# Rotary angles ahead of the masks on GpSimd, a key copy moved back, merged transfers, high products first in the up-projection

## The chip, the cores and the metric

The kernel runs on one core of a Trainium2 chip. Five engines work side by side, each through its own row of instructions in order: TensorE (PE: matmuls and transposes; PEld is its loading of weights), VectorE (DVE), ScalarE (ACT), GpSimd (Pool) and SyncE (SP, which here only issues transfers). An instruction waits for semaphores that other engines or transfers raise, and what stands behind it on its engine waits with it.

The metric is the device time in microseconds (us). The kernel before took 402.79 us, the median of three runs (402.75, 402.79 and 403.62). The times inside the program come from one profiled execution.

## What is computed

One decoder layer on 256 tokens of width 1024: RWKV-7 time mixing and an attention branch with rotary angles run on one normalised input, are merged with gates, projected, and followed by a gated MLP with a short convolution. Cut to what the change touches:

```python
def partial_rope(x, positions):
    inv_freq = ROPE_THETA ** (-jnp.arange(half, dtype=jnp.float32) / half)
    ang = positions.astype(jnp.float32)[..., None] * inv_freq
    cos = jnp.cos(ang)[:, :, None, :]
    sin = jnp.sin(ang)[:, :, None, :]
    ...
def rwkv7_time_mix(z, ...):                       # kk: normalised keys
    kk = kk / jnp.maximum(jnp.sqrt(jnp.sum(kk * kk, axis=-1, keepdims=True)), 1e-12)
    def step(state, inp):                         # a scan over the tokens
        sa = jnp.einsum('bhvk,bhk->bhv', state, a_t)
        state = (state * w_t[:, :, None, :] + sa[..., None] * b_t[:, :, None, :]
                 + v_t[..., None] * k_t[:, :, None, :])
    ...
def conv_ffn(h, w_up, conv_w, conv_b, w_down):
    u = h @ w_up
    a, b = u[..., :D_FF], u[..., D_FF:]
    a = lax.conv_general_dilated(a, ...) + conv_b  # causal, 3 wide, per channel
    return (jax.nn.gelu(a, approximate=False) * b) @ w_down
```

## The kernel before

**Products in halves.** All weights and inputs are float32. The kernel splits each operand into a high part, rounded to the matmul's own format, and the low rest, and sums three products: high by high, high weight by low input, low weight by high input. Weights come in pieces of 128 x 1024 through SP into `raw` (four buffers). ACT (or DVE, three times) casts a piece to `whi` (L299, L301), DVE subtracts to get `wlo` (L310, three buffers), and TensorE takes both. `hx` holds the split input: `hh` and `hl`. In `wst` a piece with four blocks k gives, for each half m of the columns, eight high products (L346 with `hh`, L348 with `hl`, in turn) and then four low ones (L351).

**Order.** The first steps are written out by hand. Then two or three threads of work, written as generators (`chain` for RWKV-7, `bulk` for projections, gates and attention), hand over to each other by costs and delays that they name; a scheduler places each instruction, and `tc.issue_after(x)` puts one behind another. What comes out is one fixed row of instructions for each engine.

**Pool.** Early it makes `ident` and loads small parameters. `late_consts` then fills the constants: `bones`, `gmask`, `cmask` (L141), and `m16`, `m32` (L142 to L148), both shown as `m` in the profile. Behind them stands the arithmetic of the rotary angles in `rope_tables`: positions (`posi`) to float (`posf`, L208), times the frequencies `inv` (`ang`, L214), whole turns taken off in three steps (L218 to L228), clipped (L230). ACT makes `trig`, the sines and cosines, of `ang` (L232).

**DVE.** `masks` makes `rowf` from `ident` and multiplies `m16` by it (L154). This instruction was put behind the scan `L` (L666) with `issue_after`; on DVE it stands in front of `zs` (L414, the scaled output of a projection) and the `wlo` of the next weights. ACT and DVE make the keys `zk` from `zs` (L419, L420).

**RWKV-7.** ACT squares the keys (`sq`, L682), TensorE sums them (`pss`, L690), and the keys are normalised. DVE writes scaled keys into `KB` (L734, L737), which are transposed (`pk`, L761). Later the inverse of a triangular matrix is needed for chunks of 64 tokens; its blocks in `Xb` go through memory (`d`) into the block-diagonal `X` (L874, L879), which TensorE reads (`pp` L917, `px` L934).

**MLP.** For each of 11 groups j, `up()` makes two products: `acc`, from which `an` (L1482), `cv`, GELU and `hb` follow, and `at`, which multiplies `cv` (L1499). `down` (L1464 to L1468) adds the group's share to four sums `f0` to `f3`. In the first group `token_scale` works out the scale of the second norm: `rs` through ACT's square root (L1441), `rx` on DVE (L1443), and the transposes `prs` on TensorE (L1445).

Of the kernel before, what the change touches and what calls it, by code (L numbers as in the profile page):

```python
# [9 lines left out]
F32 = mybir.dt.float32  # L10
# [18 lines left out]
HALF = 8  # L29
# [8 lines left out]
def body(tc, x, positions, norm1_g, w_in, rwkv_mu, w_decay_up, decay_bias, w_aaa_up,  # L38
# [5 lines left out]
    with ctx:  # L44
# [25 lines left out]
        def acc(name="acc"):  # L70
            return ps.tile([128, 512], F32, name=name, tag="acc", bufs=3)
# [40 lines left out]
        def keep_warm(n):  # L112

            for _ in range(n):
                pe.matmul(idle[:, 0:256], ones[:, 0:128], ones[:, 0:256], start=True, stop=True)
# [16 lines left out]
        def late_consts():  # L132
            pool.memset(rst.rearrange("p (c i) -> p c i", i=64)[:, :, 0:1], 0.0)
            pool.memset(mhalf, -0.5)
            pool.memset(bones, 0.0)
            for q in range(2):
                pool.memset(bones[64 * q:64 * q + 64, 64 * q:64 * q + 64], 1.0)
            pool.tensor_copy(bonr, bones)
            pool.tensor_scalar(gmask[:, 0:64], jl[:, 0], 0.0, None, op0=OP.is_gt)
            pool.tensor_scalar(gmask[:, 64:128], jl[:, 1], 0.0, None, op0=OP.is_ge)  # L140
            pool.tensor_scalar(cmask, jp, 0.0, NEG, op0=OP.is_gt, op1=OP.mult)  # L141
            pool.memset(m16, 0.0)  # L142
            pool.memset(m32, 0.0)
            for q in range(4):
                o = 32 * (q % 2)
                pool.memset(m16[32 * q:32 * q + 32, o:o + 16], 1.0)
                if q % 2:
                    pool.memset(m32[32 * q:32 * q + 32, 0:32], 1.0)  # L148
# [22 lines left out]
        def col(i):  # L171
            return par[:, i:i + 1]
# [17 lines left out]
        loads += [(wdu[0:64], w_decay_up[0]), (wdu[64:128], w_aaa_up[0])]  # L190
        for i, g in enumerate((q_norm_g, k_norm_g)):
            loads.append((gqk[:, i], bass.AP(tensor=g.tensor, offset=g.offset, ap=[[0, 128], [1, 64]])))
        loads.append((posi, positions[0].rearrange("(t p) -> p t", p=128)))

        def small_loads(n, eng=None):
            for _ in range(n):
                (eng or nc.gpsimd).dma_start(*loads.pop(0))

        last_exp = []
        scans = []  # L200
        trig = cst.tile([128, 2, 2, HALF], F32, name="trig")
        turn = cst.tile([128, 2, 2, 2, 2, HALF], F32, name="turn")
        gcol = cst.tile([128, 1], F32, name="gcol")

        def rope_tables():
            ang = sb.tile([128, 2, 2, HALF], F32, name="ang")
            posf = sb.tile([128, 2], F32, name="posf")
            pool.tensor_copy(posf, posi)  # L208
            inv = sb.tile([128, HALF], F32, name="inv")
            fr = (500000.0 ** (-np.arange(HALF) / HALF)).astype(np.float32)  # L210
            for i in range(HALF):
                dve.memset(inv[:, i:i + 1], float(fr[i]))
            for t in range(2):
                pool.tensor_scalar(ang[:, 0, t], inv, posf[:, t:t + 1], None, op0=OP.mult)  # L214
            turns = sb.tile([128, 2, 2, HALF], F32, name="turns")
            part = sb.tile([128, 2, 2, HALF], F32, name="part")
            MAGIC = 12582912.0
            pool.tensor_scalar(turns[:, 0], ang[:, 0], 1.0 / (2 * math.pi), None, op0=OP.mult)  # L218
            pool.tensor_scalar(turns[:, 1], turns[:, 0], 0.25, None, op0=OP.add)
            pool.tensor_scalar(turns, turns, MAGIC, None, op0=OP.add)  # L220
            pool.tensor_scalar(turns, turns, MAGIC, None, op0=OP.subtract)
            c1 = 6.28125
            c2 = float(np.float32(round((2 * math.pi - c1) * 2 ** 20) / 2 ** 20))
            c3 = 2 * math.pi - c1 - c2
            pool.tensor_copy(ang[:, 1], ang[:, 0])
            for c in (c1, c2, c3):
                pool.tensor_scalar(part, turns, -c, None, op0=OP.mult)
                pool.tensor_tensor(ang, ang, part, op=OP.add)  # L228
            pool.tensor_scalar(ang[:, 1], ang[:, 1], math.pi / 2, None, op0=OP.add)
            pool.tensor_scalar(ang, ang, 3.1415925, -3.1415925, op0=OP.min, op1=OP.max)  # L230
            with tc.issue_after(last_exp[0]):
                act.activation(trig, ang, AF.Sin)  # L232
# [100 lines left out]
        def run(gen):  # L333
            for _ in gen:
                pass
# [87 lines left out]
        def first_steps():  # L423
# [13 lines left out]
            dve.memset(ones[:, 0:256], 1.0)  # L437
            dve.memset(eps1[:, 0:1], NORM_EPS)
            dve.memset(eps1[:, 1:2], N * NORM_EPS)
            keep_warm(12)  # L440
            pool.iota(jp, pattern=[[1, 128]], base=0, channel_multiplier=-1)
            pool.tensor_scalar(ident, jp, 0.0, None, op0=OP.is_equal)
# [3 lines left out]
            wdu_at = len(loads) - 5  # L446
            for _ in range(2):
                nc.sync.dma_start(*loads.pop(wdu_at))
            load_pair(early[1])
# [68 lines left out]
            both(2, 4)  # L518
            pool.memset(rst, 1.0)
            pool.memset(cmask, 0.0)  # L520
            pts.append(acc("xt").rearrange("p (k t c) -> p k t c", k=2, t=2))
            raw1, k1, c1 = raws.pop(0)
            hi1, lo1 = tiles("whi"), tiles("wlo")
# [79 lines left out]
        def ch16(t):  # L603
            return t.rearrange("p a (c i) -> p (a c) i", i=64)
# [43 lines left out]
        def chain():  # L648
# [30 lines left out]
            zk = zs["k"]  # L679
            sq = by("sq")  # L680
            for ct in range(4):
                act.activation(sq[:, ct], zk[:, ct], AF.Square, scale=col(KK_ + ct))  # L682
            yield 0, 4.5
            p = [chp("pss") for _ in range(2)]
            for t in range(2):
# [35 lines left out]
            def kbv(q, a):  # L721
                return KB[:, 64 * q:64 * q + 2048].rearrange("p (u a i) -> p u a i", a=2, i=64)[:, :, a]
# [8 lines left out]
            bb = av  # L731
            dve.tensor_tensor(flat(bb), flat(kk), flat(av), op=OP.mult)
            yield 0, 2.9
            dve.tensor_tensor(kbv(0, 1), ch16(bb), ch16(e3), op=OP.mult)  # L734
            for q, hs in PAR:
                with tc.issue_after(rqi):
                    last_k = dve.tensor_tensor(kbv(q, q)[hs], ch16(kp)[hs], ch16(e3)[hs], op=OP.mult).ins  # L737
                yield 0, 1.0
            yield from need("r", zs)
# [5 lines left out]

            G = [b8(f"G{q}", [128, 16, 128]) for q in range(2)]
            d1 = dr.tile([128, 256], F32, name="d1")
            d2 = dr.tile([8, 2, 16, 256], F32, name="d2")
# [112 lines left out]
            for n, o in ((4, 0), (4, 8), (8, 0)):  # L861
# [7 lines left out]
                if n == 4:  # L869
                    yield 0, 1.8  # L870
            dve.tensor_copy(Xb[:, 1, 0:256].rearrange("p (n i) -> p n i", n=16),
                            X0[:, 0:256].rearrange("p (i n) -> p n i", i=16))
            for xx in range(2):
                nc.sync.dma_start(d2[:, xx], Xb[:, xx, 0:256])  # L874

            def to_x(eng, side, x, us_, src):
                b = src[1]
                q0 = bsl(side).start + 16 * b
                eng.dma_start(X[q0:q0 + 16, x, us_, 16 * b:16 * b + 16],  # L879
                              d2[4 * src[0] + b, x, src[2]].rearrange("u (i n) -> i u n", i=16))  # L880

            for q in range(2):
                for b in range(4):
                    to_x((nc.sync, nc.gpsimd)[q], q, 0, slice(0, 16), (q, b, slice(0, 16)))
            for q in range(2):
                for b in range(4):
                    for a in range(2):
                        to_x((nc.sync, nc.gpsimd)[a], a, 1, slice(8 * q, 8 * q + 8), (q, b, slice(8 * a, 8 * a + 8)))

            def bank(nm):
                return chp(nm).rearrange("p (u n) -> p u n", u=8)
# [404 lines left out]
        def bulk():  # L1302
# [51 lines left out]
            while not last_exp:  # L1354
                yield 0, 0.5
            rope_tables()
            yield from queries()
# [91 lines left out]


        def up(bank=acc):
            p = bank()
            run(wst(p, 2, hh, hl))
            return p.rearrange("p (m s) -> p m s", m=2)

        def down(j, hb):
            for i in range(2):
                wh, wl = weights()
                st = j == 0 and i == 0
                for f in range(4):  # L1460
# [7 lines left out]
                    pe.matmul(fin[f], hb[:, 0, i, ts], wl[:, 0, cs], start=False, stop=False,  # L1468
                              skip_group_check=f == 3)

        prev = []
        for j in range(11):
# [81 lines left out]
```

## Time and profile before

| | us |
|---|---|
| median of the runs | 402.79 |
| the profiled execution | 402.01 |
| its span, first to last instruction | 400.2 |
| TensorE busy | 394.3 |
| VectorE busy | 301.9 |
| ScalarE busy | 237.3 |
| GpSimd busy | 49.5 |

The span lies 1.8 us below the time of the execution that it belongs to. In a row of a timeline the first number is the start in us, the second the time that it covers (that of several instructions where it ends in x2 or more); then come the engine, the line, the operation, what it writes and reads, and in brackets how long the engine stood idle before it and what ended that. Starts can lie a little before the end of the instruction ahead, since they overlap. In a list of waits the numbers are the total, the count and the longest. In the view of one tile, a row gives the shortest, median and longest duration in ns.

### The profile page before, as it was taken

To read this page: it belongs to the slowest core of one execution; us is meant where nothing else is said; L and a number is where in the kernel's file an instruction comes from. 1 tells how busy PE (TensorE), PEld (TensorE's weight loads), DVE (VectorE), ACT (ScalarE), POOL (GpSimd) and SP (SyncE) were. 2 spreads that over 40 slices of the span, in tenths; PEclk is the share of its full clock that TensorE was granted. 3 is DMA by queue.
4 is the path that set the end of the run, shared out by engine and by line. 5 is a ranking of instruction groups with operands and counts; after the bars stand their busy time and mean duration, and the time that the engine had idled before them with its cause. 6 is when DMAs were issued, how large, how long until landed. Compare 5 with 4: busy or idle time off the path is not lost.

```text
span 400.2 us, 9024 instructions
## 1 busy us (share of the span) xinstructions
PE 394.3 (99%) x3633; PEld 365.9 (91%) x3633; DVE 301.9 (75%) x508; ACT 237.3 (59%) x411; POOL 49.5 (12%) x87
## 2 busy tenths in 40 slices
PE   8999999999999999999999999999999999999996
PEld 6899999898999989999888999999999999999995
DVE  4989989899868989688875885765757667576583
ACT  5899477494747686635554874554545546455350
POOL 8888000010600021120000000000000000000000
PEclk9999999999999999999999999999999999999999
DMA  8943397554694333555661765666665565665612
GB/s 255 323 147 86 86 305 219 139 153 124 145 292 128 108 98 128 201 162 185 199 195 56 261 206 184 196 189 195 191 208 186 185 208 168 204 211 163 208 52 105
DMA packets 60589, 70.58 MB, mean 176 GB/s; under 512 B 7377, under 2 KB 51287, under 8 KB 60548
## 3 DMA queue, kind: packets, MB, share of 16 engines
q1 hardware_dynamic: 58116, 69.17, 56.1%
q10 hardware_dynamic: 1632, 0.59, 0.6%
q8 instruction: 28, 0.46, 0.5%
q0 software_dynamic: 800, 0.26, 0.4%
q14 instruction: 13, 0.11, 0.1%
HBM read 68.56 MB, written 1.44 MB: 175 GB/s over the span
## 4 chain that ended last, share of the span: by engine, by line
PE 85%; POOL 4%; DMA 4%; DVE 3%; ACT 1%; issue 1%; SPq 0%; POOLq 0%
PE acc L346 11%; PE acc L351 11%; PE acc L348 11%; PE at L351 5%; PE at L346 5%; PE at L348 5%; PE f L1468 5%; PE f L1466 5%; PE f L1464 5%; PE acc L367 4%; PE acc L371 4%; PE acc L368 4%; DMA posi<-in_positions_dram 2%; PE acc L1322 2%; PE pq L1323 1%; DMA p<-in_aaa_bias_dram 1%
## 5 line engine op out<-in xcount | busy, mean ns | idle before, releaser
L299 ACT CAST whi<-raw 128x1024 fp32r<-128x1024 f32 (+1 forms) x122 | 124.5, 1025 | 111.3 <-PE acc L348 44.0
L310 DVE TENSOR_TENSOR wlo<-raw,whi 128x1024 fp32r<-128x1024 f32 (+1 forms) x122 | 144.6, 1188 | 37.7 <-PE f L1468 14.4
L346 PE MATMUL acc<-hx,whi 128*128 128x256 f32 x400 | 99.4, 284 | 0.0
L348 PE MATMUL acc<-hx,whi 128*128 128x256 f32 x400 | 97.1, 279 | 0.0
L346 PEld LDWEIGHTS acc<-hx,whi 128*128 128x128 f32 x400 | 75.4, 188 | 2.4 <-issue 0.8
L348 PEld LDWEIGHTS acc<-hx,whi 128*128 128x128 f32 x400 | 75.4, 188 | 0.4
L351 PE MATMUL acc<-hx,wlo 128*128 128x256 f32 x400 | 62.3, 278 | 0.2 <-DVE rs L1440 0.2
L351 PEld LDWEIGHTS acc<-hx,wlo 128*128 128x128 f32 x400 | 53.2, 188 | 0.4 <-DVE wlo L310 0.4
L346 PE MATMUL at<-hx,whi 128*128 128x256 f32 x176 | 42.4, 278 | 0.0
L348 PE MATMUL at<-hx,whi 128*128 128x256 f32 x176 | 42.3, 277 | 0.0
L348 PEld LDWEIGHTS at<-hx,whi 128*128 128x128 f32 x176 | 33.1, 188 | 0.0
L346 PEld LDWEIGHTS at<-hx,whi 128*128 128x128 f32 x176 | 33.1, 188 | 0.0
L1468 PE MATMUL f<-wlo,hb 128*128 128x512 f32 x80 | 31.6, 395 | 0.0
L1466 PE MATMUL f<-whi,hb 128*128 128x512 f32 x80 | 31.4, 393 | 0.0
L1464 PE MATMUL f<-whi,hb 128*128 128x512 f32 x80 | 31.2, 390 | 0.0
L351 PE MATMUL at<-hx,wlo 128*128 128x256 f32 x176 | 27.3, 277 | 0.0
L351 PEld LDWEIGHTS at<-hx,wlo 128*128 128x128 f32 x176 | 23.3, 188 | 0.0
L1466 PEld LDWEIGHTS f<-whi,hb 128*128 128x128 f32 x80 | 15.0, 188 | 3.1
L1468 PEld LDWEIGHTS f<-wlo,hb 128*128 128x128 f32 x80 | 15.1, 189 | 3.0
L1464 PEld LDWEIGHTS f<-whi,hb 128*128 128x128 f32 x80 | 15.0, 188 | 2.9
L1482 DVE TENSOR_TENSOR an<-acc,rsb 128x512 f32<-128x512 f32 x11 | 7.6, 692 | 13.1 <-PE acc L351 12.9
L1499 DVE TENSOR_TENSOR cv<-cv,at 128x256 f32<-128x256 f32 x22 | 8.3, 417 | 10.2 <-PE at L351 9.9
(359 smaller groups left out, 696.2 us busy)
## 6 DMA issues: line engine op xcount, KB each, us to landing
raw<-in_w_ffn_up_dram SPq DMA_DIRECT2D x44, 512.0 KB, 3.6
raw<-in_w_in_dram SPq DMA_DIRECT2D x33, 512.0 KB, 4.7
raw<-in_w_ffn_down_dram SPq DMA_DIRECT2D x22, 512.0 KB, 3.4
raw<-in_w_out_dram SPq DMA_DIRECT2D x8, 512.0 KB, 4.2
raw<-in_w_in_dram SPq DMA_DIRECT2D x8, 272.0 KB, 2.9
early<-in_w_in_dram SPq DMA_DIRECT2D x2, 1024.0 KB, 8.1
raw<-in_w_branch_b_dram SPq DMA_DIRECT2D x4, 512.0 KB, 3.5
raw<-in_w_branch_a_dram SPq DMA_DIRECT2D x4, 512.0 KB, 3.4
```

The lines of the kernel that those rows point to most:

```text
L299: act.copy(wide(hi, k, c), spread(raw, k, c))
L310: eng.tensor_tensor(wide(lo, k, c), spread(raw, k, c), wide(hi, k, c).bitcast(F32), op=OP.subtract)
L346: pe.matmul(om, wh[:, k, ms], xh[:, k0 + k], start=k0 + k + m == 0, stop=False, skip_group_check=True)
L348: pe.matmul(om, wh[:, k, ms], xl[:, k0 + k], start=False, stop=False, skip_group_check=True)
L351: pe.matmul(om, wl[:, k, ms], xh[:, k0 + k], start=False, stop=k0 + k == nk - 1 and m == n - 1, skip_group_check=True)
L367: pe.matmul(ps_[t], xh[:, K, ts], wh[:, k], start=K == 0, stop=False)
L368: pe.matmul(ps_[t], xl[:, K, ts], wh[:, k], start=False, stop=False)
L371: pe.matmul(ps_[t], xh[:, K, ts], wl[:, k], start=False, stop=K == nk - 1)
L1464: pe.matmul(fin[f], hb[:, 0, i, ts], wh[:, 0, cs], start=st, stop=False, skip_group_check=f == 3)
L1466: pe.matmul(fin[f], hb[:, 1, i, ts], wh[:, 0, cs], start=False, stop=False, skip_group_check=f == 3)
L1468: pe.matmul(fin[f], hb[:, 0, i, ts], wl[:, 0, cs], start=False, stop=False, skip_group_check=f == 3)
L1499: dve.tensor_tensor(cv, cv, pb[:, m], op=OP.mult)
```

## The change

It has five parts.

1. `rope_tables` is split. `rope_angles`, the arithmetic on Pool, is called in `late_consts` ahead of `cmask`, `m16` and `m32`; the positions are loaded earlier, by a call of `small_loads(1)` in the first steps. `rope_tables` keeps `trig`, now behind the last `sq` instead of the exponential, and the products behind it.
2. The `KB` copy of one half of the keys (q = 1) is issued behind the `KB` copy of L734.
3. The blocks of `Xb` are stored by one transfer of 128 x 256 and two of 8 x 8 x 256, and loaded by eight transfers on each of SP and Pool instead of twelve.
4. `up` no longer calls `wst`: for each piece of weights it does 16 high products, for both halves m, and then eight low ones.
5. In `down`, the low product of `f3` for i = 1 is made in two halves of 256 columns.

```diff
             pool.tensor_scalar(gmask[:, 64:128], jl[:, 1], 0.0, None, op0=OP.is_ge)
+            rope_angles()
             pool.tensor_scalar(cmask, jp, 0.0, NEG, op0=OP.is_gt, op1=OP.mult)
             pool.memset(m16, 0.0)
...
-        loads.append((posi, positions[0].rearrange("(t p) -> p t", p=128)))
+        loads.insert(12, (posi, positions[0].rearrange("(t p) -> p t", p=128)))
...
-        def rope_tables():
+        def rope_angles():
             posf = sb.tile([128, 2], F32, name="posf")
             pool.tensor_copy(posf, posi)
...
-            with tc.issue_after(last_exp[0]):
+
+        def rope_tables():
+            with tc.issue_after(last_sq[0]):
                 act.activation(trig, ang, AF.Sin)
...
             pool.memset(cmask, 0.0)
+            small_loads(1)
...
-            dve.tensor_tensor(kbv(0, 1), ch16(bb), ch16(e3), op=OP.mult)
+            kbi = dve.tensor_tensor(kbv(0, 1), ch16(bb), ch16(e3), op=OP.mult).ins
             for q, hs in PAR:
-                with tc.issue_after(rqi):
+                with tc.issue_after((rqi, kbi)[q]):
...
-            for xx in range(2):
-                nc.sync.dma_start(d2[:, xx], Xb[:, xx, 0:256])
...
+            nc.sync.dma_start(d2, Xb[:, 0, 0:256])
+            for q in range(2):
+                nc.sync.dma_start(d3[:, :, q].rearrange("b a u m -> (b a) u m"), Xb[half(q), 1, 0:256])
             for q in range(2):
                 for b in range(4):
...
+                    (nc.sync, nc.gpsimd)[q].dma_start(X[q0:q0 + 16, 0, :, 16 * b:16 * b + 16],
+                                                      d2[4 * q + b].rearrange("u (i n) -> i u n", i=16))
+            for b in range(4):
+                for a in range(2):
...
+                    (nc.sync, nc.gpsimd)[a].dma_start(X[q0:q0 + 16, 1, :, 16 * b:16 * b + 16],
+                                                      d3[b, a].rearrange("q u (i n) -> i (q u) n", i=16))
...
         def up(bank=acc):
-            p = bank()
-            run(wst(p, 2, hh, hl))
-            return p.rearrange("p (m s) -> p m s", m=2)
+            p = bank().rearrange("p (m s) -> p m s", m=2)
+            for k0 in (0, 4):
+                wh, wl = weights()
+                for w, xx in ((wh, (hh, hl)), (wl, (hh,))):
+                    for m in range(2):
+                        for k in range(4):
+                            for x_ in xx:
+                                pe.matmul(p[:, m], w[:, k, m * 128:m * 128 + 128], x_[:, k0 + k],
...
+                    for c in ((0, 512),) if f < 3 or i == 0 else ((0, 256), (256, 512)):
+                        pe.matmul(fin[f][:, c[0]:c[1]], hb[:, 0, i, ts],
```

Three places in the rows of instructions. First, Pool's row around the masks; `m_89` is `m16`, `m_90` is `m32`. Before:

```order
L140 TENSOR_SCALAR gmask<-jl 128x64
L141 TENSOR_SCALAR cmask<-jp 128x128
L142 MEMSET m_89 128x64
L143 MEMSET m_90 128x64
L146 MEMSET m_89 32x16 x2
L148 MEMSET m_90 32x32
L146 MEMSET m_89 32x16 x2
L148 MEMSET m_90 32x32
L208 CAST posf<-posi 128x2
L214 TENSOR_SCALAR ang<-inv,posf 128x8 x2
```

And the end of the angles and the masks behind them after the change:

```order
L228 TENSOR_TENSOR ang<-ang,part 128x32
L229 TENSOR_SCALAR ang<-ang 128x16
L230 TENSOR_SCALAR ang<-ang 128x32
L142 TENSOR_SCALAR cmask<-jp 128x128
L143 MEMSET m_89 128x64
L144 MEMSET m_90 128x64
L147 MEMSET m_89 32x16 x2
L149 MEMSET m_90 32x32
L147 MEMSET m_89 32x16 x2
L149 MEMSET m_90 32x32
L240 TENSOR_TENSOR gcol<-par 128x1
```

Between `gmask` and `cmask` now stand all 16 instructions of the angles, L212 to L230.

Second, DVE's row of the changed kernel from the scan `L` on:

```order
L672 SCALAR_TENSOR_TENSOR L<-rst,sg 128x1024
L303 CAST whi<-early 128x1024
L155 TENSOR_SCALAR m_89<-m_89,rowf 128x64
L416 TENSOR_TENSOR zs<-acc,rsb_107 128x512
L312 TENSOR_TENSOR wlo<-early,whi 128x1024
L680 COPY PC<-sg 128x16
L422 SCALAR_TENSOR_TENSOR zk<-zs,par,zk 128x255 x2
L312 TENSOR_TENSOR wlo<-early,whi 128x1024
```

Nothing moved here: before, the same instructions stand in the same order (L666, L301, L154, L414, L310, L674, L420, L310). The product of L155 reads and writes `m16`, so it waits for the last of its memsets on Pool.

Third, TensorE's row in the first group of the MLP. Before, the second piece of `acc`'s weights ends and `at` begins with:

```order
L351 MATMUL acc<-hx,wlo 128x256 x4
L346 MATMUL at<-hx,whi 128x256
L348 MATMUL at<-hx,whi 128x256
L346 MATMUL at<-hx,whi 128x256
L348 MATMUL at<-hx,whi 128x256
L346 MATMUL at<-hx,whi 128x256
L348 MATMUL at<-hx,whi 128x256
L346 MATMUL at<-hx,whi 128x256
L348 MATMUL at<-hx,whi 128x256
L351 MATMUL at<-hx,wlo 128x256 x4
```

After the change, from the second piece of `acc` on:

```order
L1457 MATMUL acc<-hx,whi 128x256 x16
L1457 MATMUL acc<-hx,wlo 128x256 x8
L1457 MATMUL at<-hx,whi 128x256 x15
L1443 MATMUL prs<-ident,rx_3245 128x128 x2
L1444 MATMUL prs<-ident,p_2838 128x88
L1457 MATMUL at<-hx,whi 128x256
L1457 MATMUL at<-hx,wlo 128x256 x8
```

The low products stand eight high ones later in each piece. The transposes `prs` come behind 15 matmuls of `at`; before, they came behind 14 (eight high, four low, two high).

More of the change, by code (lines that the diff above doesn't have):

```diff
@@ L199, in body @@
         last_exp = []
+        last_sq = []
         scans = []
@@ L203, in body @@
         gcol = cst.tile([128, 1], F32, name="gcol")
-        def rope_tables():
-            ang = sb.tile([128, 2, 2, HALF], F32, name="ang")
+        ang = sb.tile([128, 2, 2, HALF], F32, name="ang")
+        inv = sb.tile([128, HALF], F32, name="inv")
+        def rope_angles():
             posf = sb.tile([128, 2], F32, name="posf")
             pool.tensor_copy(posf, posi)
[L209 to L212, printed above, removed]
             for t in range(2):
@@ L439, in first_steps @@
             dve.memset(eps1[:, 1:2], N * NORM_EPS)
+            fr = (500000.0 ** (-np.arange(HALF) / HALF)).astype(np.float32)
+            for i in range(HALF):
+                dve.memset(inv[:, i:i + 1], float(fr[i]))
             keep_warm(12)
@@ L445, in first_steps @@
             small_loads(8)
-            wdu_at = len(loads) - 5
+            wdu_at = 1
             for _ in range(2):
@@ L681, in chain @@
             for ct in range(4):
-                act.activation(sq[:, ct], zk[:, ct], AF.Square, scale=col(KK_ + ct))
+                last_sq[:] = [act.activation(sq[:, ct], zk[:, ct], AF.Square, scale=col(KK_ + ct)).ins]
             yield 0, 4.5
@@ L747, in chain @@
             d1 = dr.tile([128, 256], F32, name="d1")
-            d2 = dr.tile([8, 2, 16, 256], F32, name="d2")
+            d2 = dr.tile([8, 16, 256], F32, name="d2")
+            d3 = dr.tile([4, 2, 2, 8, 256], F32, name="d3")
             Tb = sb.tile([128, 272], F32, name="Tb")
@@ L872, in chain @@
                             X0[:, 0:256].rearrange("p (i n) -> p n i", i=16))
-            for xx in range(2):
-                nc.sync.dma_start(d2[:, xx], Xb[:, xx, 0:256])
[L876 to L880, printed above, removed]
+            nc.sync.dma_start(d2, Xb[:, 0, 0:256])
+            for q in range(2):
+                nc.sync.dma_start(d3[:, :, q].rearrange("b a u m -> (b a) u m"), Xb[half(q), 1, 0:256])
             for q in range(2):
                 for b in range(4):
[L884 to L888, printed above, removed]
+                    q0 = bsl(q).start + 16 * b
+                    (nc.sync, nc.gpsimd)[q].dma_start(X[q0:q0 + 16, 0, :, 16 * b:16 * b + 16],
+                                                      d2[4 * q + b].rearrange("u (i n) -> i u n", i=16))
+            for b in range(4):
+                for a in range(2):
+                    q0 = bsl(a).start + 16 * b
+                    (nc.sync, nc.gpsimd)[a].dma_start(X[q0:q0 + 16, 1, :, 16 * b:16 * b + 16],
+                                                      d3[b, a].rearrange("q u (i n) -> i (q u) n", i=16))
             def bank(nm):
@@ L1352, in gate_input @@
                     dve.tensor_tensor(xgh[ws, 1], xg[ws, 1], xgh[ws, 1].bitcast(F32), op=OP.subtract)
-            while not last_exp:
+            while not last_sq:
                 yield 0, 0.5
@@ L1451, in up @@
         def up(bank=acc):
-            p = bank()
-            run(wst(p, 2, hh, hl))
-            return p.rearrange("p (m s) -> p m s", m=2)
+            p = bank().rearrange("p (m s) -> p m s", m=2)
[6 more added lines that the diff above has]
+                                pe.matmul(p[:, m], w[:, k, m * 128:m * 128 + 128], x_[:, k0 + k],
+                                          start=k0 + k + m == 0 and x_ is hh and w is wh,
+                                          stop=k0 + k + m == 8 and w is wl, skip_group_check=True)
+            return p
         def down(j, hb):
@@ L1467, in down @@
                               skip_group_check=f == 3)
-                    pe.matmul(fin[f], hb[:, 0, i, ts], wl[:, 0, cs], start=False, stop=False,
-                              skip_group_check=f == 3)
+                    for c in ((0, 512),) if f < 3 or i == 0 else ((0, 256), (256, 512)):
+                        pe.matmul(fin[f][:, c[0]:c[1]], hb[:, 0, i, ts],
+                                  wl[:, 0, hf * 512 + c[0]:hf * 512 + c[1]], start=False, stop=False,
+                                  skip_group_check=f == 3)
         prev = []
```

## The prediction, made before the changed kernel ran

> **What bounds the kernel now.** I read the page's busy times first, then the list of what TensorE (PE) waited for, then the chain that ended last, then the timelines of GpSimd (Pool) and VectorE (DVE) from 16 to 36 us.
>
> ```profile
> PE 394.3 (99%) x3633; PEld 365.9 (91%) x3633; DVE 301.9 (75%) x508; ACT 237.3 (59%) x411; POOL 49.5 (12%) x87
> ```
> ```profile
> PE idle L115 <- DVE eps L438: 1.2, 1, 1.2
> ...
> PE pss L690 <- ACT sq L682: 0.3, 1, 0.3
> ```
>
> TensorE is busy for 394.3 of 400.2 us, its longest wait is the first 1.2 us, and the Pool chain that the change moves shows only behind the second row. So an edit gains at most the few tenths that a stall costs, and loses whatever new stall it makes.
>
> ```profile
> 14.66 6.67 DMA posi<-in_positions_dram
> ...
> 34.38 1.14 POOL ang L230
> ...
> 36.22 0.76 PE pss L690 x40
> ```
>
> The chain of waits runs from the load of the positions through Pool's 14 us of angle arithmetic into `trig`, the fourth `sq` and `pss`. It looks like a long critical path, but TensorE had other matmuls all the while, so only what `pss` waits for at its end is to be had.
>
> **Angles ahead of the masks.** The rows of Pool before, the constant `ident` (early, undisturbed) first:
>
> ```profile
> 1.18 0.57 POOL L442 TENSOR_SCALAR ident<-jp 128x128 f32<-128x128 int32 x1
> ...
> 9.33 0.20 POOL L520 MEMSET cmask<- 128x128 f32 x1
> ...
> 14.66 0.74 POOL L197 DMA_DIRECT2D posi<-in_positions_dram  x1
> ...
> 18.43 1.65 POOL L141 TENSOR_SCALAR cmask<-jp 128x128 f32<-128x128 int32 x1
> ...
> 20.57 0.25 POOL L146 MEMSET m<- 32x16 f32 x2
> ...
> 21.46 0.84 POOL L208 CAST posf<-posi 128x2 f32<-128x2 int32 x1 [0.59 <-DMA posi<-in_positions_dram]
> 22.40 3.04 POOL L214 TENSOR_SCALAR ang<-inv,posf 128x8 f32<-128x8 f32 x2
> ...
> 28.74 0.30 POOL L227 TENSOR_SCALAR part<-turns 128x32 f32<-128x32 f32 x1
> 29.13 1.17 POOL L228 TENSOR_TENSOR ang<-ang,part 128x32 f32<-128x32 f32 x1
> ...
> 33.98 0.31 POOL L229 TENSOR_SCALAR ang<-ang 128x16 f32<-128x16 f32 x1
> ```
>
> The last memset of `m16` ends at 20.57 + 0.25 = 20.82. Here is DVE:
>
> ```profile
> 17.55 0.72 DVE L301 CAST whi<-early 128x1024 fp32r<-128x1024 f32 x1
> 18.33 1.23 DVE L310 TENSOR_TENSOR wlo<-raw,whi 128x1024 fp32r<-128x1024 f32 x1
> 19.48 0.51 DVE L420 SCALAR_TENSOR_TENSOR xg<-zs,par,xg 128x255 f32<-128x255 f32 x1
> 19.91 2.35 DVE L310 TENSOR_TENSOR wlo<-early,whi 128x1024 fp32r<-128x1024 f32 x2
> 22.18 2.28 DVE L666 TENSOR_TENSOR_SCAN L<-rst,sg 128x1024 f32<-128x1024 bf16 x1
> 24.38 0.66 DVE L301 CAST whi<-early 128x1024 fp32r<-128x1024 f32 x1
> 24.96 0.24 DVE L154 TENSOR_SCALAR m<-m,rowf 128x64 f32<-128x64 f32 x1
> ...
> 25.73 1.21 DVE L310 TENSOR_TENSOR wlo<-early,whi 128x1024 fp32r<-128x1024 f32 x1
> ...
> 28.96 1.23 DVE L310 TENSOR_TENSOR wlo<-early,whi 128x1024 fp32r<-128x1024 f32 x1 [0.46 <-ACT whi L299]
> ...
> 33.70 0.48 DVE L420 SCALAR_TENSOR_TENSOR zk<-zs,par,zk 128x255 f32<-128x255 f32 x1
> ```
>
> DVE multiplies `m16` by `rowf` at 24.96, 4.1 us after Pool is done, so it costs nothing today. The change leaves this instruction where it stands in DVE's row, but puts 16 angle instructions and `cmask` between Pool's `gmask` and the memsets. DVE works in order: `zs`, two `wlo` and all that follows stand behind it. So the question is **when Pool reaches the last `m16` memset**, which I call T.
>
> Pool starts the chain at about 17.7: it reached `cmask` at 18.43, and the 0.74 us issue of `posi` now lies in an earlier gap. The positions are there by then: issued at 9.5, behind the early memset of `cmask`, they need 6.67 us, hence 16.2. From 17.7 to 25.0 the rows pair off: `posf` ends at 22.30 with the second `wlo` (22.26), and the two `ang` (3.04 us) last as long as the scan and the CAST behind it, where an undisturbed Pool instruction of this size takes 0.30 and, from start to start (28.74 to 29.13, 33.98 to 34.38), 0.40. So I give Pool one instruction for each of DVE's large ones: `posf`, `ang`, `ang`, L218, L219 and L220 against CAST, `wlo`, `wlo`, `wlo`, scan, CAST (`xg`, 0.5 us long, goes with its neighbours).
>
> At 25.0 DVE then stands still, and Pool is alone with ten small instructions (L221, L225, three pairs L227/L228, L229, L230): 10 x 0.39 = 3.9. `cmask` follows at the price of `ident`, 0.57 and 0.1 between; then the memsets at 20.82 - 20.08 = 0.74. T = 25.0 + 3.9 + 0.7 + 0.7 = **30.3**. Bounds: with 0.30 each, T = 29.4; with two instructions fewer done by 25.0, 31.1; with every angle instruction as long as before and `cmask` at 1.65, see the rivals.
>
> The Trainium skill, "SBUF — State Buffer", section "Who interferes with whom", says that a DVE instruction with two SBUF inputs, or a copy in its two-port mode, holds a port pair that a GpSimd instruction reading SBUF has to wait for. By that rule Pool is quick once DVE stands still, as my sum has it; the trace agrees (L228 ends at 30.30, DVE's `wlo` at 28.96 + 1.23 = 30.19). If instead Pool's instructions were as long by nature as they were before, it would be the second rival below.
>
> What TensorE loses, from its weight loads (PEld) and `pss`:
>
> ```profile
> 29.10 0.54 PEld L351 LDWEIGHTS acc<-hx,wlo 128*128 128x128 f32 x4
> ...
> 31.92 0.54 PEld L351 LDWEIGHTS acc<-hx,wlo 128*128 128x128 f32 x4
> ```
> ```profile
> 35.43 0.53 PE L690 MATMUL pss<-bones,sq 64*64 64x1 f32 x24
> ```
> ```profile
> 217.58 1.21 DVE L310 TENSOR_TENSOR wlo<-raw,whi 128x1024 fp32r<-128x1024 f32 x1
> ```
> ```profile
> 218.85 0.30 PEld L351 LDWEIGHTS acc<-hx,wlo 128*128 128x128 f32 x2 [0.43 <-DVE wlo L310]
> ```
>
> The last two rows give the hand-over: `wlo` ends at 218.79, the load starts 0.06 later. DVE's shift is 30.3 - 24.96 = 5.34. The `wlo` of 25.73 to 26.94 then ends at 32.28, and its load, at 29.10 before, starts at 32.34: **+3.24**. The next `wlo` ended at 30.19 against a load at 31.92; its chain runs through `zs`, ACT's `zk` and ACT's cast, which had a little idle time, so I take its shift as 5.1: 35.29 + 0.06 against 31.92 + 3.24, another **+0.2**. Behind it the lead grows and nothing waits until `pss`.
>
> `pss` is where the angles should pay:
>
> ```profile
> 35.54 0.23 ACT L232 ACTIVATE trig<-ang 128x32 f32<-128x32 f32 x1 [0.85 <-POOL ang L230]
> ```
>
> `pss` began at 35.43, went on until 35.76, and the rest came at 36.22, 0.46 later, since `sq` stood behind `trig`, which waited 0.85 for Pool. After the change the fourth `sq` goes first, but it reads the last `zk` (33.70 to 34.18 on DVE), which the stall moves by about 5: 39.2, `sq` to 39.7, against a TensorE that has moved by 3.4 to 39.2. The wait is then about 0.6 instead of 0.46, **+0.1**: what is late next is DVE, not Pool. Bounds: -0.46 without a stall, +0.5 if DVE's lag does not shrink at all.
>
> From T = 27.1 on (32.28 - 3.24 - 1.97 of `m`, `zs`, `wlo`) each us of T is a us of TensorE.
>
> **The key copy moved back.**
>
> ```profile
> 40.20 1.22 DVE L737 TENSOR_TENSOR KB<-kp,L 64x1024 f32<-64x1024 f32 x1
> ```
>
> 1.22 us of DVE go from 40.20 to behind the `KB` copy of 49.27; the transposes that read it start at 58.52. That leaves 8 us, so it costs 0; it even returns 1.22 us to DVE, which runs late just there, so I add no further wait after 40 us.
>
> **The inverse's transfers merged.**
>
> ```profile
> L934 PE MATMUL px<-P,X x64: 218/220/241, 115.1 to 116.0; 64*64 64x32 f32 x64
> ...
> L879 SPq DMA_DIRECT2D X<-d x12: 337/430/454, 102.6 to 107.8; - x12
> ```
>
> Four loads fewer on each of SP and Pool, one store more: at 0.43 us an issue the weights queued behind them on SP come about 1.3 us sooner. No wait of TensorE is listed there, so the gain is 0, and a loss would need `X` to come later, though it has fewer issues ahead of it: 0, within 0.2 either way.
>
> **High products first in the up-projection, one down product split.**
>
> ```profile
> 222.54 0.41 PE L1445 MATMUL prs<-ident,rx 128*128 128x128 f32 x2
> ```
> ```profile
> 222.10 0.29 DVE L1443 COPY rx<-rs 128x256 f32<-128x256 f32 x1
> ```
>
> The 0.43 wait for `wlo` at 218.85 goes, because eight more high products stand ahead of it. But `prs` waits for `rx` (to 222.39), which comes out of a busy ACT and does not move. So TensorE waits at `prs` instead, having done one matmul more: **-0.1**. With an earlier `rx` it would be -0.4. Later groups show no wait before; low products ahead of `an` put the activation about 1 us later, up to +0.5 if `hb` misses its matmul. The split replaces one 512-column product by two of 256 ten times, equal columns: 0.
>
> **Sum.** 3.24 + 0.2 + 0.1 - 0.1 = +3.4 us. The profiled execution took 402.01, 0.8 below the median of 402.79, so a like one would take 405.4, and the forecast for the median is **406.2**.
>
> **The rivals.**
>
> *Pool gets through in time* (not slower). If Pool's instructions slip in beside DVE's, as L227 and L229 did (0.30 and 0.31 us), T could be below 27.1. Then only the gains are left, -0.46 and -0.1: 402.2. Against it: from 25.0 to 27.1 only `cmask`, the memsets and two small instructions fit, so 14 angle instructions instead of six would have to be done by 25.0, beside DVE's long ones. Chance 0.09.
>
> *Pool stays slow though DVE stands still*: angle chain 35.5 - 21.5 = 14.0, less 0.4 of other work, then 1.65 and 0.74, from 17.7: T = 33.7, 3.4 later, 409.6. Against it: L227 and L229 show that an instruction alone takes 0.30. Chance 0.08.
>
> *The stall slows TensorE's clock.*
>
> ```profile
> PEclk9999999999999999999999999999999999999999
> ```
> ```profile
> 1.19 2.74 PE L115 MATMUL idle<-ones 128*128 128x256 bf16 x12 [1.19 <-DVE eps L438]
> ```
>
> The page grants nearly the full clock in every slice. At the start, after idling, 256 columns took 2.74/12 = 0.23 us; four of L351 take 0.54. If the idle 3.24 us bring that pace back for as long as these twelve, half of 2.7 us is lost, up to 2 with a longer spell: 407.9. The wait must be long enough for that, which no row here decides; chance 0.1. The Trainium skill, "TensorE: Matmul & The Clock Gate", Part 1, puts the window at about 3.4 us, so that a wait like mine would mostly just escape.
>
> *The order in the up-projection bites*: `hb` late by 0.5 in one or more of the 11 groups, on top of the stall: 407 to 408. Chance 0.07.
>
> **How the numbers follow.** The forecast, T between 29.4 and 31.1, has 0.66: 405.3 to 407.0. I widen by 0.6 for its small terms, 404.7 at the lower end, and at the upper end take in the clock and the up-projection, 408.3. Outside are the first two rivals. A difference of 0.2% (0.8 us) is about what can be told from no change. Slower than that, above 403.6: all but the first rival, 0.91. Its 402.2 lies 0.2 above the bound of 402.0, so of its 0.09 I give 0.06 to within 0.2% and 0.03 to faster.
>
> **What would show it.** DVE idle for 4.4 to 6.2 us ahead of `m<-m,rowf`, released by Pool's memset; Pool's small instructions at 0.3 from 25 us on; TensorE waiting about 3.2 us for `wlo` near 29 and ACT no longer waiting for `ang`; `prs` still waiting near 222.5 us plus the shift, with no wait for `wlo` ahead of it; `X` without a wait. The forecast is wrong if DVE passes `m` before 27.1, or if TensorE had more low products in hand than the loads at 29.10 and 31.92 show.

## The result, and the profile after

The changed kernel took 407.47 us (median of four runs, 406.99 to 407.96); the kernel before took 403.06 beside it. The ratio is 1.0107 (95% interval 1.009 to 1.0123): 1.1% slower, 4.4 us by the medians. The forecast was 406.2 (404.7 to 408.3). The profiled execution took 406.99 with a span of 405.2, 5.0 more than the span before.

First the rows on which the forecast rested, in the changed kernel: Pool's timeline from the angles to the masks.

```profile
16.17 0.57 POOL L212 CAST posf<-posi 128x2 f32<-128x2 int32 x1
16.84 1.76 POOL L214 TENSOR_SCALAR ang<-inv,posf 128x8 f32<-128x8 f32 x2
...
24.87 0.67 POOL L227 TENSOR_SCALAR part<-turns 128x32 f32<-128x32 f32 x1
25.62 0.25 POOL L228 TENSOR_TENSOR ang<-ang,part 128x32 f32<-128x32 f32 x1
...
28.02 0.66 POOL L142 TENSOR_SCALAR cmask<-jp 128x128 f32<-128x128 int32 x1
...
29.17 0.25 POOL L147 MEMSET m<- 32x16 f32 x2
```

DVE's timeline; the bracket gives its idle time and what ended it:

```profile
24.71 0.67 DVE L303 CAST whi<-early 128x1024 fp32r<-128x1024 f32 x1
29.45 0.25 DVE L155 TENSOR_SCALAR m<-m,rowf 128x64 f32<-128x64 f32 x1 [4.08 <-POOL m L147]
29.62 0.68 DVE L416 TENSOR_TENSOR zs<-acc,rsb 128x512 f32<-128x512 f32 x1
30.22 1.22 DVE L312 TENSOR_TENSOR wlo<-early,whi 128x1024 fp32r<-128x1024 f32 x1
```

TensorE's weight load that takes this `wlo`, and two matmuls a little later:

```profile
31.49 0.53 PEld L353 LDWEIGHTS acc<-hx,wlo 128*128 128x128 f32 x4 [1.98 <-DVE wlo L312]
```
```profile
32.78 0.42 PE L348 MATMUL acc<-hx,whi 128*128 128x256 f32 x1
32.99 0.42 PE L350 MATMUL acc<-hx,whi 128*128 128x256 f32 x1
```

DVE stood still for 4.08 us in front of `m`, released by the last memset of `m16`, and TensorE waited for `wlo`. Then comes what the forecast had only as a rival: the matmuls start 0.21 us apart instead of 0.113. The windows of 4 us (length, busy us and count for each engine, then the granted clock) show it:

```profile
28.00:32.00 4.00, 2.22 (x20) 2.02 (x19) 2.46 (x5) 1.66 (x3) 1.72 (x12) 1.00 0.00 0
32.00:36.00 4.00, 4.00 (x23) 4.00 (x23) 3.31 (x4) 4.00 (x7) 0.00 (x0) 0.57 0.03 6
36.00:40.00 4.00, 4.00 (x82) 3.87 (x83) 3.81 (x6) 3.14 (x6) 0.00 (x0) 1.00 0.46 118
```

The granted clock (the share of full speed that TensorE got) is 0.57 from 32 to 36 us. TensorE counts as busy there, so a list of waits doesn't show this loss.

Behind it, ACT and then TensorE, at `pss` and at `prs`:

```profile
38.43 0.51 ACT L688 ACTIVATE sq<-zk,par 128x256 f32<-128x256 f32 x1 [0.84 <-DVE zk L422]
...
40.25 0.23 ACT L234 ACTIVATE trig<-ang 128x32 f32<-128x32 f32 x1
```
```profile
39.23 0.93 PE L696 MATMUL pss<-bones,sq 64*64 64x1 f32 x52
```
```profile
226.60 0.41 PE L1443 MATMUL prs<-ident,rx 128*128 128x128 f32 x2
```

`sq` now waits for `zk` instead of `trig`, and `pss` runs through without a wait.

Following the same matmul through both traces gives how late TensorE is at each place:

| place | before | after | later by |
|---|---|---|---|
| first product with the late `wlo`, had it not waited (the one ahead, 29.44, + 0.11) | 29.21 | 29.55 | 0.3 |
| the same product as it was | 29.21 | 31.49 | 2.3 |
| first product with the next `wlo` | 32.04 | 35.96 | 3.9 |
| first `pss` | 35.43 | 39.23 | 3.8 |
| `prs` | 222.54 | 226.60 | 4.1 |
| first matmul of `down` | 238.21 | 242.15 | 3.9 |
| first 256-column `f` product at the end | 395.53 | 400.21 | 4.7 |

So the wait is 1.9 us and the slow clock 1.65 (3.92 less 2.28). 0.1 comes back until `pss`, since the products behind 36 us went at 0.113 us instead of 0.118, and 0.45 inside `pss`: the first product behind it starts at 40.42 instead of 37.07, 3.35 later. Between `pss` and `prs` 0.7 us is lost in small pieces, and in the down-projection 0.75 more, evenly over the groups behind the first.

### The profile page after: what moved, and what is told of

Read it like the earlier page. It is cut to its first block, busy times and chain, and to the rows that moved or that the text cites. A ratio compares the mean times of both kernels' runs of the same rounds, so it can differ in the third digit from the quotient of the medians.

```text
span 405.2 us, 9036 instructions
## 1 busy us (share of the span) xinstructions
PE 397.4 (98%) x3643; PEld 368.1 (91%) x3643; DVE 302.4 (75%) x508; ACT 239.9 (59%) x411; POOL 42.6 (11%) x83
## 4 chain that ended last, share of the span: by engine, by line
PE 83%; DVE 5%; POOL 4%; DMA 4%; ACT 3%; issue 1%; ACTq 0%; SPq 0%; DVEq 0%; POOLq 0%
PE at L1457 14%; PE acc L1457 14%; PE acc L348 7%; PE acc L353 7%; PE acc L350 6%; PE f L1476 5%; PE f L1472 5%; PE f L1470 5%; PE acc L369 4%; PE acc L370 4%; PE acc L373 4%; DVE wlo L312 1%; DMA p<-in_aaa_bias_dram 1%; DMA x<-in_x_dram 1%; DMA raw<-in_w_in_dram 1%
## 5 line engine op out<-in xcount | busy, mean ns | idle before, releaser
L301 ACT CAST whi<-raw 128x1024 fp32r<-128x1024 f32 (+1 forms) x122 | 124.6, 1025 | 97.8 <-PE f L1472 27.2
L348 PE MATMUL acc<-hx,whi 128*128 128x256 f32 x224 | 57.6, 292 | 0.2 <-DVE whi L554 0.2
L350 PE MATMUL acc<-hx,whi 128*128 128x256 f32 x224 | 55.5, 283 | 0.0
L348 PEld LDWEIGHTS acc<-hx,whi 128*128 128x128 f32 x224 | 43.0, 192 | 2.4 <-issue 0.8
L1457 PE MATMUL acc<-hx,whi 128*128 128x256 f32 x352 | 44.3, 278 | 0.0
L1457 PE MATMUL at<-hx,whi 128*128 128x256 f32 x352 | 44.0, 278 | 0.0
L350 PEld LDWEIGHTS acc<-hx,whi 128*128 128x128 f32 x224 | 43.1, 192 | 0.0
L1457 PEld LDWEIGHTS acc<-hx,whi 128*128 128x128 f32 x352 | 42.1, 188 | 0.0
L1457 PEld LDWEIGHTS at<-hx,whi 128*128 128x128 f32 x352 | 41.9, 188 | 0.0
L353 PE MATMUL acc<-hx,wlo 128*128 128x256 f32 x224 | 35.5, 282 | 1.8 <-DVE wlo L312 1.8
L353 PEld LDWEIGHTS acc<-hx,wlo 128*128 128x128 f32 x224 | 30.2, 191 | 2.2 <-DVE wlo L312 2.2
L1476 PE MATMUL f<-wlo,hb 128*128 128x512 f32 (+1 forms) x90 | 31.6, 370 | 0.0
L1457 PE MATMUL acc<-hx,wlo 128*128 128x256 f32 x176 | 23.7, 277 | 0.0
L1457 PE MATMUL at<-hx,wlo 128*128 128x256 f32 x176 | 23.7, 277 | 0.0
L1457 PEld LDWEIGHTS at<-hx,wlo 128*128 128x128 f32 x176 | 21.7, 188 | 0.0
L1457 PEld LDWEIGHTS acc<-hx,wlo 128*128 128x128 f32 x176 | 21.7, 188 | 0.0
L1476 PEld LDWEIGHTS f<-wlo,hb 128*128 128x128 f32 x90 | 17.0, 188 | 3.9
```

Of the source, the lines that this page charges most:

```text
L301: act.copy(wide(hi, k, c), spread(raw, k, c))
L348: pe.matmul(om, wh[:, k, ms], xh[:, k0 + k], start=k0 + k + m == 0, stop=False, skip_group_check=True)
L350: pe.matmul(om, wh[:, k, ms], xl[:, k0 + k], start=False, stop=False, skip_group_check=True)
L353: pe.matmul(om, wl[:, k, ms], xh[:, k0 + k], start=False, stop=k0 + k == nk - 1 and m == n - 1, skip_group_check=True)
L1457: pe.matmul(p[:, m], w[:, k, m * 128:m * 128 + 128], x_[:, k0 + k], start=k0 + k + m == 0 and x_ is hh and w is wh, stop=k0 + k + m == 8 a ...
L1476: pe.matmul(fin[f][:, c[0]:c[1]], hb[:, 0, i, ts], wl[:, 0, hf * 512 + c[0]:hf * 512 + c[1]], start=False, stop=False, skip_group_check=f ...
```

## The experiments

Each ran in five rounds beside the kernel before; times are medians. All keep the whole computation.

### e1, e2, e4: the wait and the clock

e1 moves the call behind the memsets:

```diff
-            rope_angles()
             pool.tensor_scalar(cmask, jp, 0.0, NEG, op0=OP.is_gt, op1=OP.mult)
...
                     pool.memset(m32[32 * q:32 * q + 32, 0:32], 1.0)
+            rope_angles()
```

> The changed kernel with one edit: the angles stand behind the memsets of m16 and m32 on Pool again; the early load of the positions and all else stay. Theory (the wait of DVE's m<-m,rowf for Pool costs TensorE about 2.0 us at its next low product, and the idle time halves its clock for 3.4 us, 1.7 us more): both go, no idle time of DVE before m, granted clock 1.00, about 403.9 us against 407.5. Rival (the loss comes from other parts, the split product, the key copy, the load of the positions): little changes, above 406.5.

403.43 us against 403.08, ratio 1.0004 (0.9988 to 1.002). DVE's `m` starts without a wait, and so does TensorE's load that waited, in the two timelines:

```profile
25.36 0.25 DVE L155 TENSOR_SCALAR m<-m,rowf 128x64 f32<-128x64 f32 x1
```
```profile
29.18 0.53 PEld L353 LDWEIGHTS acc<-hx,wlo 128*128 128x128 f32 x4
```

e2 leaves Pool alone and moves the instruction that waits; `last_k` is the last `KB` copy:

```diff
-        def masks():
+        def masks(late):
...
-            with tc.issue_after(scans[0]):
+            with tc.issue_after(late):
                 dve.tensor_scalar(m16, m16, rowf, None, op0=OP.mult)
...
-            masks()
+            masks(last_k)
```

> The changed kernel with one edit: DVE multiplies m16 by rowf behind the last KB copy instead of behind the scan; Pool's order stays as changed. Theory (only the place of the waiting instruction matters): as e1, about 403.9 us, with Pool's chain ending near 33 us since DVE no longer stands still. Rival (Pool's angles beside DVE's work hold DVE up by themselves): the low product near 31 us still waits by 1 us or more, above 405.

403.03 us, ratio 1.0001 (0.9984 to 1.0019). The loss of 4 us goes with either edit, so Pool's early angles harm nothing by themselves: the harm is done by the instruction that waits for Pool, with DVE's work behind it. The timeline of Pool in e2 also shows what Pool pays beside a working DVE:

```profile
29.57 1.69 POOL L142 TENSOR_SCALAR cmask<-jp 128x128 f32<-128x128 int32 x1
```

The same `cmask` took 0.66 us in the changed kernel, while DVE stood still.

e4 makes the wait shorter, with the last two angle instructions behind the masks:

```diff
                     pool.memset(m32[32 * q:32 * q + 32, 0:32], 1.0)
+            rope_clip()
...
+        def rope_clip():
             pool.tensor_scalar(ang[:, 1], ang[:, 1], math.pi / 2, None, op0=OP.add)
             pool.tensor_scalar(ang, ang, 3.1415925, -3.1415925, op0=OP.min, op1=OP.max)
```

> The changed kernel with the last two angle instructions on Pool (L229, L230) behind the memsets: the masks are ready about 0.65 us earlier, and TensorE should wait about 1.3 instead of 2.0 us. If the clock falls after any wait of over 1 us: the same slow stretch of 3.4 us, about 406.8. If the wait of 2.0 us only just reached it: no slow stretch, granted clock 1.00, about 405.1.

405.94 us, ratio 1.0074 (1.0046 to 1.0102). The weight load that waits, the window from 32 to 36 us, and `pss`:

```profile
30.98 0.53 PEld L356 LDWEIGHTS acc<-hx,wlo 128*128 128x128 f32 x4 [1.56 <-DVE wlo L315]
```
```profile
32.00:36.00 4.00, 4.00 (x36) 3.86 (x34) 3.40 (x5) 4.00 (x7) 0.00 (x0) 1.00 0.02 6
```
```profile
37.34 0.53 PE L699 MATMUL pss<-bones,sq 64*64 64x1 f32 x24
38.47 0.76 PE L699 MATMUL pss<-bones,sq 64*64 64x1 f32 x40 [0.61 <-ACT sq L691]
```

The clock stays at 1.00 behind an idle time of 1.56 us, where it fell behind 1.98. And here `pss` does wait, from 37.67 to 38.47, 0.8 us, as the prediction had it. The expectation left this out; the time is 0.8 above its 405.1 for a clock that holds. In the changed kernel the clock was slow, and TensorE came to `pss` late enough for `sq` to be there: the slow clock covered this wait, and so its net price was less than 1.65. Behind `pss` TensorE is 2.24 us late in e4 (its next product starts at 39.31) and 3.35 in the changed kernel; 0.5 of the difference is the load that starts earlier (30.98 instead of 31.49), so the slow clock cost about 0.6 net, or 1.0 by the medians (1.5 less 0.5).

That 1.56 us is too short for the clock to fall is not shown, though. e3, below, keeps the whole wait, and its trace has the slow spell at another place behind it. Here are the two spells as windows of their own, the changed kernel first:

```profile
32.23:35.63 3.40, 3.40 (x19) 3.40 (x18) 2.94 (x4) 3.40 (x5) 0.00 (x0) 0.50 0.03 7
```
```profile
34.43:37.84 3.41, 3.41 (x18) 3.41 (x17) 3.08 (x4) 3.41 (x7) 0.00 (x0) 0.51 0.01 2
```

Both last 3.41 us, but the first begins 0.74 us after the late load (31.49), the second 1.49 after it (32.94, with an idle time of 2.33). In both traces the spell begins a whole number of times 3.41 us after the trace's record of the clock first has it full: eight times in the changed kernel (from 4.91 us), seven in e3 (from 10.53). If the clock is decided upon at such steps, the idle time within one step counts. It was 1.98 us in the changed kernel and 1.93 in e3. In e4 the steps, counted from 6.80 us, have a border at 30.69: they cut its idle time, from 29.42 to 30.98, into 1.28 and 0.28. So e4 doesn't say what 1.56 us within one step would do. Nor does the clock fall each time: two of e3's six executions have a mean clock of 0.998 and 0.999 and took 406.54 and 406.31 us, the other four 0.995 or 0.996 and 408.00 to 408.23. All four of the changed kernel lie at 0.994 to 0.996; the 30 of e1, e2 and e4 lie at 0.998 or more. Of the 23 of the kernel before beside them, four have 0.996 too, and at what place is not known.

### e3, e5, e7, e8: what made the down-projection slower

In the trace of before the 24 products of a down block follow each other from 254.71 to 260.20, in the changed kernel from 258.65 to 264.23:

```profile
254.71 0.39 PE L1464 MATMUL f<-whi,hb 128*128 128x512 f32 x1
...
260.20 0.28 PE L346 MATMUL acc<-hx,whi 128*128 128x256 f32 x1
```
```profile
258.65 0.39 PE L1470 MATMUL f<-whi,hb 128*128 128x512 f32 x1
...
264.23 0.75 PE L1457 MATMUL acc<-hx,whi 128*128 128x256 f32 x5
```

That is 5.49 against 5.58 us with no wait in either. The first block takes 5.60 in both traces; all later ones differ like these two. e3 takes the split back:

```diff
-                    for c in ((0, 512),) if f < 3 or i == 0 else ((0, 256), (256, 512)):
+                    for c in ((0, 512),):
```

> The changed kernel with the low product of f3, i=1, whole again, as before. Theory A (two matmuls of 256 columns change the pace of the whole down block, 5.577 instead of 5.494 us in nine of ten groups in the traces): 0.75 us less, about 406.7. Theory B of the prediction (equal columns, equal time; the slower blocks have another cause): no change, 407.4, and blocks of 5.577 us stay.

408.05 us (ratio 1.0104, 1.0076 to 1.0132), blocks still 5.58 us (259.93 to 265.51): not the split. The next suspect was the order in the up-projection (theory U). e5 is e2 with the old `up` (`run(wst(p, 2, hh, hl))`), e8 is e5 without the split, and e7 is the kernel before with the new `up`.

> e2 (mask multiplied late) with the up-projection as before: eight high, four low products for each half. Theory U (the new order of the up-projection sets the slower pace of the down blocks that follow it): nine blocks at 5.494 us instead of 5.577, about 0.7 us less than e2, 402.4. Rival S (the two 256-column products, or where the program now stands, set it): blocks stay at 5.577 and the time at 403.0. The wait for wlo near 218 us comes back, the one at prs shrinks to 0.2: no net change from that.

> e5 without the split of the low product of f3. If the split alone slows the blocks: 5.494 us here and 5.577 in e5. If it makes no difference (e3 already says so beside the new order): both alike, whichever pace e5 has.

> The kernel before with the new order of the up-projection alone. Theory U: down blocks at 5.577 us, so 0.75 us slower less 0.1 gained at prs, about 403.7 against 403.1. Rival S: blocks stay at 5.494 and the time at 403.0.

e5: 404.13 us (ratio 1.0018, 1.0001 to 1.0036); e8: 403.68 (1.0013, 0.9997 to 1.003); both with blocks of 5.58 us. e7: 403.18 (1.0019, 0.9993 to 1.0044), blocks 5.50 (255.66 to 261.16). Theory U fell too. Two things stay open: e5 took 1.1 us more than the higher of its two expectations, and its trace, of an execution of 402.64 us, doesn't show where; and three of e7's twelve executions took 405.73 to 406.63 us at full clock, of which no trace was kept. e8 has the same matmuls in the up- and down-projection as before, and is slow there; e7 has others, and is fast. Something set before these stages had to differ.

### e6: the key copy

```diff
-                with tc.issue_after((rqi, kbi)[q]):
+                with tc.issue_after(rqi):
```

> e5 with the key copy at its early place again. Theory (the late copy stands ahead of the wlo that TensorE waits 0.22 us for near 54.5 us): that wait goes, 0.2 us less than e5. Rival (VectorE is late there for another reason): the wait stays. A difference of 0.2 us shows in the trace only, the times are expected to be the same.

404.21 us (ratio 1.0028, 1.0013 to 1.0044), and the expectation failed. The 0.22 us near 54.5 went, but TensorE now waited 0.99 us for a `wlo` just after 49 us:

```profile
50.46 0.40 PE L1320 MATMUL acc<-wlo,hx 128*128 128x288 f32 x1 [0.99 <-DVE wlo L312]
```

From e5 to e6 TensorE's `pss` starts 1.28 us later (35.10 and 36.39), but the `zs` behind the copy on DVE 2.46 (40.71 and 43.17). So DVE has no room for the copy near 40 us when `pss` is early, and moving the copy back goes with the earlier `trig`. (The product of `m16` moved with it, since it is tied to the last copy; the copy is 1.22 us of DVE, the product 0.26.) The medians of e5 and e6 differ by 0.08 us only, so this is read from the traces alone.

### e9 to e12: the place of `hb`

The split of `rope_tables` also changes where tiles lie. `ang` and `inv` are allocated earlier than before, `posf`, `turns` and `part` too, and large tiles allocated behind them move up by 160 or 448 bytes per partition. Among those that move by 448 is `hb`, the stationary operand of the down-projection. e10 does this alone: in the kernel before, the five tiles are allocated ahead of the threads. Of the four tiles that TensorE reads in the up- and down-projection (`hx`, `whi`, `wlo`, `hb`), only `hb` gets another address by that.

```diff
+        ang = sb.tile([128, 2, 2, HALF], F32, name="ang")
+        posf = sb.tile([128, 2], F32, name="posf")
...
         threads = [["chain", chain(), 0.0], ["bulk", bulk(), 0.0]]
```

> The kernel before with its five small angle tiles allocated ahead of the large ones: hb stands 448 bytes higher, as in the changed kernel, and every engine's instructions are the same and in the same order. Theory H: nine down blocks go from 5.494 to 5.577 us, 0.75 us slower than before, about 403.8. Rival: 403.1, blocks unchanged.

```profile
255.72 0.39 PE L1464 MATMUL f<-whi,hb 128*128 128x512 f32 x1
...
261.29 0.28 PE L341 MATMUL acc<-hx,whi 128*128 128x256 f32 x1
```

5.57 us for the block, as in the changed kernel, in the same instructions. The time was 403.47 us (1.0008, 0.9994 to 1.0023), where 0.75 more was expected; the interval takes in 0 to 0.9 us, so that the price is shown by the trace only.

e9 goes the other way: e2 with the five tiles as slices of an unused constant tile, which puts `hb` back. e11 moves it by 224 bytes, and e12 is e9 without the split.

```diff
-        cst.tile([128, 200], F32, name="gap")
+        gap = cst.tile([128, 200], F32, name="gap")
...
-        inv = sb.tile([128, HALF], F32, name="inv")
+        inv = gap[:, 32:40]
```

> e2 (mask multiplied late, all else as changed) with the five small angle tiles as slices of an unused constant tile, so that they no longer push the tiles behind them: hb, the stationary operand of the down-projection, stands 448 bytes lower per partition, where it stood before the change. No instruction moves. Theory H (the place of hb sets the pace of the down blocks): 5.494 us instead of 5.577 in nine blocks, 0.75 us less than e2, about 402.3. Rival (something else of the change sets the pace, or chance between builds): blocks stay at 5.577, 403.0.

> e9 with hb 224 bytes higher instead of 0 or 448. Theory H in the form that an address counts by its place within some block of bytes: a third pace is possible, no number forecast; the form that only the distance to other tiles counts gives no number either. The rival of no influence: as e9.

> e9 without the split of the low product of f3: the angles early, the mask multiplied late, the new order of the up-projection, hb where it stood before. If the split is what puts the matmuls of the up-projection into the slow pace at this place of hb (0.1178 instead of 0.1133 us each in e9): down blocks at 5.494 us and up stretches at 0.1133, as in e7, so e2 less 0.75, about 402.3, which would be 0.8 below the kernel before. If only the place of hb together with the rest of the change does it: as e9, about 407.

e9 missed widely: 406.99 us (1.0096, 1.0075 to 1.0116). e11: 407.35 (1.0101, 1.0081 to 1.0121). e12: 402.56 (0.9996, 0.9978 to 1.0013), with blocks of 5.49 us. Here are 16 high products behind the second down block, in e9 and in e12:

```profile
263.55 2.05 PE L1457 MATMUL acc<-hx,whi 128*128 128x256 f32 x16
265.43 1.11 PE L1457 MATMUL acc<-hx,wlo 128*128 128x256 f32 x8
```
```profile
263.12 1.98 PE L1457 MATMUL acc<-hx,whi 128*128 128x256 f32 x16
264.93 1.07 PE L1457 MATMUL acc<-hx,wlo 128*128 128x256 f32 x8
```

16 products take 1.88 us (263.55 to 265.43) in e9 and 1.81 in e12, 0.118 and 0.113 each. In e9 all stretches of the up-projection keep the slow pace, and its down blocks take 5.60: together, over nine groups, that is the loss. e11 has the slow pace too, and blocks of 5.62. So the split costs 4.4 us (406.99 less 402.56) where `hb` stands as before, and nothing that shows where it stands 448 bytes higher (e3 against the changed kernel, e8 against e5); 224 bytes higher, without the split, was not run.

The up-projection's products read neither `hb` nor what the split changes, so the slow pace doesn't come from their own operands. Nor is it new: between `prs` and the first down block the products go at 0.118 us in all fourteen traces, in e12 too (1.89 us for 16):

```profile
232.72 2.05 PE L1457 MATMUL at<-hx,whi 128*128 128x256 f32 x16
234.61 1.11 PE L1457 MATMUL at<-hx,wlo 128*128 128x256 f32 x8
```

Behind the first down block they go at 0.113 in twelve traces and stay at 0.118 in e9 and e11. So the split at these two places of `hb` doesn't slow the up-projection down; with it the faster pace doesn't come. Why, the traces don't say: TensorE waits for nothing there.

e12, the early angles, the late mask, the new `up` and no split, is as fast as before within its interval; none of these kernels beats it.

## Why the prediction was right

- **The wait.** DVE stopped in front of `m`, and TensorE paid, as forecast; e1 and e2 show it from both sides. T was sized at 30.3 and was 29.4, at the low bound. Pool reached `posf` at 16.17, not 17.7: its `gmask` instructions took 0.4 us each instead of 1.2, beside other work of DVE than before. So eight angle instructions were done by 25.0 instead of six, and eight were left, not ten. From 25.6 on these went as the sum had them (0.21 to 0.29 us each, 0.34 from start to start), and so did `cmask` (0.66) and the memsets. The load that the sum moved by 3.24 us moved by 2.39 (29.10 to 31.49), and TensorE's idle time ahead of it was 2.0. The +0.2 for the next `wlo` didn't show, since TensorE came late at its slow clock; in e4 it was 0.1.
- **The clock.** It was given a chance of 0.1 and left out of the sum. It happened, and it cost 1.65 us by the starts of the same matmuls, less what it covered at `pss`. The Trainium skill, "TensorE: Matmul & The Clock Gate", Part 1, puts the idle window at about 3.4 us; here 1.98 us was enough, and the measurement decides. The prediction's sentence that a wait of 3.2 us would mostly escape was wrong.
- **`pss`.** The term +0.1 came out at about -0.45, since the slow clock covered the wait. Without it, in e4, `pss` waits 0.8 us where it waited 0.46 before: +0.3, the mechanism as forecast. The gain of the earlier `trig` is real only where DVE isn't late: in e1 and e2 `pss` has no wait.
- **The key copy and the transfers.** Taken at 0. In the changed kernel a low product near 58.8 us waits 0.2 us for `wlo`, with the copy ahead of that on DVE, and TensorE is 0.4 us later behind it; `pg` waits 0.3 near 105 us for a cast. What part of these is the copy's was not settled. `X` has no wait of TensorE, as forecast.
- **`prs`.** As forecast: the wait for `wlo` ahead of it went, the one for `rx` came in its place (0.3 us instead of 0.2), and the net gain from `prs` to the first `down` was 0.1.
- **The split** was taken at 0, and in the changed kernel it is (e3). But the down-projection lost 0.75 us, which no term held: the place of `hb`. The prediction looked at rows of instructions only, and no row moved for it.

So the sign and the mechanism were right, and that 3.4 us of the sum come close to 4.4 of the medians is in part luck: errors of both signs cancel. By the traces, whose spans differ by 5.0, the sum had the wait 1.3 us too long (3.24 against the 1.94 by which it made TensorE later), 0.2 for a second wait that didn't show and `pss` 0.55 too high. It left out 1.65 for the clock, 0.75 for the place of `hb`, 0.7 in small pieces between `pss` and `prs`, and 0.3 at each end of the program. The first 29 us differ from run to run by more than that: in e3, with the same instructions up to there, the product that waits would have started at 30.64 instead of 29.55.

## What to carry to other kernels

Moving work on an idle engine means reading which in-order engine waits for what is now behind it; an instruction of 0.25 us that waits costs everything queued behind it. If a sum makes the matmul engine idle for about 2 us, as here, give the slow clock behind it a real share in the sum: it came in all four executions of the changed kernel and in four of six of e3. And a change that allocates small tiles at another point moves large ones: compare addresses as well as rows of instructions.

## What the runs showed of the hardware

- **Idle time and clock.** 1.98 us of idle TensorE, behind 12 us without a wait, brought the granted clock to 0.50 from 32.23 to 35.63 us, with matmuls 0.21 us apart; in e3 2.33 us did, from 34.43 to 37.84. The spell lasted 3.41 us both times and began 0.74 and 1.49 us after work resumed. Behind 1.56 us, in e4, the clock held; two falls are too few for a rule.
- **Pool beside DVE.** The same `cmask` took 0.66 us with DVE idle and 1.69 beside it, and the second L227 0.29 in the changed kernel and 1.31 in e2.
- **Two paces of TensorE without a wait.** 256-column products went at 0.113 or 0.118 us at full clock, both in one trace; down blocks behind the first took 5.49, 5.58, 5.60 or 5.62 us, by where `hb` stands and by whether the last product of a block is split. Moving `hb` by 448 bytes cost 0.08 us a block without the split; with the split, the old place cost 4.4 us in all.
